# Cross samples' third and fourth key fetches a step sooner, and projection weights from the fifth pair on loaded by ScalarE's queue

## The chip, the cores and the metric

The kernel runs on one core of a Trainium2 chip. The metric is the device time of one execution in microseconds (us). A run of the kernel before takes 1438.98 us (median of three, 1438.52 to 1439.62). One execution was profiled; the views quoted below are all of that one.

The engines are named as the profile names them: PE (TensorE, matrix products), PEld (its weight loads), DVE (VectorE), ACT (ScalarE), POOL (GpSimd) and SP (SyncE). SPq and ACTq stand for the instructions with which SP and ACT issue DMA transfers. Each engine works through its own list in order and waits at the head of it: an instruction that waits holds everything behind it on its engine, DMA issues included.

## The reference

One inference step of one mixer layer, for a prompt group (1 x 1024 tokens) and a sample group (8 x 1 token) with the same weights, all in float32. Cut to what matters here:

```python
h = rmsnorm(x, norm_gain)
proj = h @ w_in                                   # 1024 x 10256, one combined input projection
q, k, v, gla_g, a_lr, u, pool_g, xq, xg, merge = split(proj)
o, S = gla_chunked(q, k, v, log_a, S0)            # branch A: gated linear attention, 4 heads
br_gla = rmsnorm(o, gla_gain) * silu(gla_g)
br_pool = multiscale_pool(u, ...) * silu(pool_g)  # branch B: trailing means of 2/4/8/16 tokens
# branch C: cross-attention, 4 heads of 256, into 256 memory tokens
s = einsum('bthd,bmhd->bhtm', xq, mk) / 16
br_x = einsum('bhtm,bmhd->bthd', softmax(s), mv) * silu(xg)
y = sum_n(sigmoid(merge_n) * (branch_n @ w_branch[n])) @ w_out
out = rmsnorm(x + y, final_gain)
```

For the prompt, `mk` and `mv` are made from `mem_prompt`. For the 8 samples the keys and values come from a cache (`cache_mem_k`, `cache_mem_v`: 8 samples x 256 tokens x 4 heads x 256), so each sample has its own keys.

## The kernel before, in words

**The projection.** `w_in` is worked through in 40 `pairs` of 2 x 128 columns. A pair is one block product by Strassen's scheme with seven products, numbered j = 0 to 6: 11, 12, s2, s1, s3, s4 and 22 are the seven left operands, made from the four quarters a11, a12, a21, a22 of the pair's weights. Every float32 operand is split in a high part `h` (made by ACT) and a low part `l` (made by DVE: the operand less its high part), and each product of two such operands takes three matmuls (L242, L243, L244). One product is 2 halves x 4 x 3 matmuls of 128 x 258; the order of the products is `seq`: (i,1) to (i,4), then (i+1,0), then (i,5), (i,6).

**The weights' path.** A pair's weights come in two DMA transfers of 512 KB into tiles called `raw` (`Pair.load`, L296): `lo`, the first half of the rows, has a11 and a21, and `hi` has a12 and a22. There are three such buffers for all pairs. `prepare` makes the left operands three products ahead of the one that PE is given, and places the loads: `hi` of the next pair when s3 = a11 - a21 is made (j = 4), which is the last use of the buffer it takes over, and `lo` of the pair after that when a22 has been split (j = 6). In `operands`, L305 is a DVE sum or difference of quarters; `ws<-raw` of s1 = a21 + a22 is the first DVE instruction of a pair that needs its `hi`.

**The side work.** Between the half products, `fill` lets a stream of side work run: cross-attention (`cross_steps`), then gated linear attention, then pooling. Each step yields a cost, and `fill` goes on until the costs so far have caught up with the place in the projection (493 units over the slots 28 to 357, of two for each product). The side work's products go to the PSUM tiles `pz` (two buffers), the projection's to `px` (six).

**The cross samples.** For each head h, `cross_sample` first makes the scores of the 8 samples on DVE (L768, `kc<-kc,qb`: the cached keys times a query that is spread over all partitions). Keys (`kc`, four buffers) and queries (`qb`, four) are fetched for two samples at a time by `cross_keys`: fetches 0 and 1 at the end of the head before, fetch 2 after sample 2's scores (b = 2), fetch 3 after b = 4. Fetch 2 is used from b = 4, fetch 3 from b = 6. The scores then go through PE (L777), a softmax whose result is `ps` (L779, L784), PE again (L795, L804 with the cached values `vc`) and so on. The same stream carries the prompt's cross-attention: query chunks `xq` (fetched by SP, split at L226 and L227), scores, `nm` (L709), `p`, and its transposes (L724).

**What sets the order.** PE's and SP's lists stand in the order in which the program is written. DVE's, ACT's and POOL's are laid by a scheduler; `tc.issue_after(x)` makes what follows stand behind x on the same engine. In the kernel before all these loads and fetches (`raw`, `xq`, `kc`, `qb`, `vc`) are in SP's one list.

Of the kernel before, what the change touches and what calls it, by code (L numbers as in the profile page):

```python
# [18 lines left out]
P = 128  # L19
# [28 lines left out]
def trunk_kernel(ctx: ExitStack, tc: tile.TileContext,  # L48
# [3 lines left out]
    nc = tc.nc  # L52
# [13 lines left out]
    def exp_ln_table():  # L66
        load = nc.scalar.add_instruction(mybir.InstLoadActFuncSet(
            act_func_set_id=EXP_LN_SET, name=nc.get_next_instruction_name(), engine=nc.scalar.engine,
            ins=[], outs=[]))
        for i in table["others"]:  # L70
            tc.add_manual_dep(load.ins, i.ins.name, nosync, reason="table set")
        table["load"], table["others"] = load, []

    def act(out, x, func, **kw):
        i = nc.scalar.activation(out, x, func, **kw)
        if func in (AF.Sigmoid, AF.Silu):
            table["others"].append(i)
            for e in table["exps"]:
                tc.add_manual_dep(i.ins, e.ins.name, nosync, reason="table set")
        else:  # L80
            tc.add_manual_dep(i.ins, table["load"].ins.name, nosync, reason="table set")
            table["new"].append(i)
        return i
# [15 lines left out]
    def PZ():  # L99
        return ps.tile([P, 512], F32, tag="pz", name="pz", bufs=2)  # L100
# [13 lines left out]
    def R(shape, dt=F32, name="r"):  # L114

        return shaped(wk.tile([P, 512], dt, tag="ring", name=name, bufs=NR), shape)
# [7 lines left out]
    def RAW(name):  # L124
        return wk.tile([P, 4, CT], F32, tag="raw", name=name, bufs=3)
# [7 lines left out]
    def tiny(w, name="t", bufs=8):  # L133
        return wk.tile([P, 16], F32, tag="t", name=name, bufs=bufs)[:, :w]
# [83 lines left out]
    last = {}  # L218
# [68 lines left out]
    class Pair:  # L287
# [3 lines left out]
            self.src, self.dst, self.s0, self.gated, self.raw = src, dst, s0, gated, [None, None]  # L291
            self.turned = turned

        def load(self, i):
            raw = RAW("raw")
            nc.sync.dma_start(out=raw, in_=self.src.rearrange("(k p) n -> p k n", p=P)[:, 4 * i:4 * i + 4])  # L296
            self.raw[i] = raw

        def operands(self):
# [26 lines left out]
    pairs = []  # L326
# [8 lines left out]
    NPAIR = len(pairs)  # L335
# [7 lines left out]
        seq += [(i, 5), (i, 6)]  # L343
    RIGHT = ("11", "21", "t2", "t1", "t3", "22", "t4")
    AHEAD = 3
    left, prep = {}, {"n": 0}

    def prepare(n):

        while prep["n"] < min(n + 1, len(seq)):  # L350
            i, j = seq[prep["n"]]
            p = pairs[i]
            if j == 0:
                p.gen = p.operands()
            left[i, j] = next(p.gen)

            if (i, j) == (0, 1):
                pairs[1].load(0)
            if j == 4 and i + 1 < NPAIR:
                pairs[i + 1].load(1)  # L360
            elif j == 6 and i + 2 < NPAIR:
                pairs[i + 2].load(0)
            prep["n"] += 1

# [303 lines left out]
    def loaded(src, shape, name, alloc=None):  # L668
        t = (alloc or R)(shape, name=name)
        nc.sync.dma_start(out=t, in_=src)  # L670
        return t

    def column0(t, d):

        return t.rearrange("p (i d j r) -> p i d j r", i=2, d=2, j=4)[:, :, d, :, 0]

    def perm8(ap):
        return ap.rearrange("p (i j) -> p i j", i=2)
# [60 lines left out]
    def cross_scaled(h):  # L739
        xs = wk.tile([P, 16], F32, tag="xsq", name="xsq", bufs=2).rearrange("p (i b) -> p i b", i=2)  # L740
        nc.vector.tensor_scalar(xs, smp_of(S_XQ + 2 * h, 2), 1.0 / 16.0, None, op0=ALU.mult)
        cross["xs", h] = xs

    def cross_rows(h):

        xs = cross["xs", h]
        t = PZ()
        for i in range(2):
            nc.tensor.transpose(t[:NS, i * P:(i + 1) * P], xs[:, i], ident)
        qn = R([DV], name="qn")  # L750
        nc.scalar.activation(qn[:NS], t[:NS, :DV], AF.Copy)
        nc.gpsimd.dma_start(out=xq_scr[h], in_=qn[:NS])

    def cross_keys(h, b2):
        kc = [loaded(ck[2 * b2 + bb, :, h, :].rearrange("(a p) d -> p a d", p=P), [2, DV], "kc", V) for bb in range(2)]
        qb = [wk.tile([P, DV], F32, tag=t, name="qb", bufs=2) for t in ("alc", "st")]
        for bb in range(2):
            nc.sync.dma_start(out=qb[bb], in_=xq_scr[h][2 * b2 + bb].partition_broadcast(P))
        cross["kc", h, b2] = kc, qb

    def cross_sample(h):

        sc = wk.tile([P, 16], F32, tag="sc", name="sc", bufs=2)
        for b in range(NS):
            kcs, qb = cross["kc", h, b // 2]
            kc = kcs[b % 2]
            for a in range(2):
                nc.vector.tensor_tensor_reduce(kc[:, a, :], kc[:, a, :], qb[b % 2],  # L768
                                               scale=1.0, scalar=0.0, op0=ALU.mult, op1=ALU.add,
                                               accum_out=sc[:, a * NS + b:a * NS + b + 1])  # L770
            if b in (2, 4):
                cross_keys(h, b // 2 + 1)
            yield 0.7
        yield 0.5
        t = PZ()
        for a in range(2):
            nc.tensor.transpose(t[:NS, a * P:(a + 1) * P], sc[:, a * NS:(a + 1) * NS], ident)  # L777
        nm = tiny(1, "nm")[:NS]
        nc.vector.tensor_reduce(nm, t[:NS, :NM], axis=AX.X, op=ALU.max, negate=True)  # L779
        p = R([NM], name="ps")[:NS]  # L780
        sm = tiny(1, "sm")[:NS]
        act(p, t[:NS, :NM], AF.Exp, bias=nm, accum_out=sm)
        nc.vector.reciprocal(sm, sm)
        nc.vector.tensor_scalar(p, p, sm, None, op0=ALU.mult)  # L784

        def own_values(i):
            return [loaded(cv[4 * i + j, :, h, :].rearrange("(a p) d -> p a d", p=P), [2, DV], "vc", V) for j in range(4)]

        vc = own_values(0)
        if h + 1 < NH:  # L790
            cross_scaled(h + 1)
        yield 1.5
        t = PZ()
        for a in range(2):
            nc.tensor.transpose(t[:, a * NS:(a + 1) * NS], p[:, a * P:(a + 1) * P], ident[:NS, :NS])  # L795
        nc.vector.tensor_copy(pm[:, :, :, 0], t[:, :2 * NS].rearrange("p (a b) -> p a b", a=2))
        yield 1.2
        yield 0.5
        cs = R([2, DV], name="cs")
        for i in range(2):  # L800
            t = PZ()
            for a in range(2):
                for j in range(4):
                    nc.tensor.matmul(t[32 * j:32 * j + 32, :DV], lhsT=pm[:, a, 4 * i + j, :], rhs=vc[j][:, a, :],  # L804
                                     start=a == 0, stop=a == 1)
            nc.scalar.activation(cs[:, i], t[:, :DV], AF.Copy)
            if i == 0:
                vc = own_values(1)
                yield 2.2
                yield 0.5  # L810
                if h + 1 < NH:
                    cross_rows(h + 1)
                yield 1.2
                yield 0.5
        if h + 1 < NH:
            cross_keys(h + 1, 0)
        yield 2.2
        if h + 1 < NH:
            cross_keys(h + 1, 1)
        yield 0.5  # L820
        t = PZ()
        for i in range(2):
            for d in range(2):
                nc.tensor.transpose(t[:, (2 * i + d) * P:(2 * i + d + 1) * P], cs[:, i, d * P:(d + 1) * P], ident)
        for d in range(2):
            nc.vector.tensor_copy(perm8(brs[2][:, 2 * h + d]), column0(t, d))
        yield 1.2
        yield 0.5

    def cross_steps():  # L830
# [10 lines left out]
        def values(n):  # L841
            cross_values(n // 4, n % 4)

        samples = chain_of(cross_sample(h) for h in range(NH))
        cross_load(0)
        cross_fetch(0, 0)
# [412 lines left out]

    def emit(n, ahead=AHEAD):  # L1260
        prepare(n + ahead)
        if seq[n] == (28, 0):
            streams[0].rest()
            other_table()
        elif seq[n] == (36, 0):
            streams[1].rest()
        for _ in run_product(n):
            fill()
# [38 lines left out]
    with tc.issue_after(last["hi"].ins), tc.issue_after(last["lo"].ins):  # L1307
        prepare(0)
# [6 lines left out]
    with tc.issue_after(last["hi"].ins), tc.issue_after(last["lo"].ins):  # L1315
        prepare(1)
        for j in (4, 6):
            r = squares(x_t[j:j + 2], 4 + j)
            scaled(x_t[j], r[:, 0:1])
            scaled(x_t[j + 1], r[:, 1:2], True)  # L1320
        prepare(3)
# [163 lines left out]
    for hf, order in enumerate(ORDERS):  # L1485
        for tb in order:
# [23 lines left out]
            n, a = hf, 0  # L1510
            for b in ends:
# [14 lines left out]
                n, a = n + 1, b  # L1526
# [46 lines left out]
```

## Time and profile before

| what | value |
|---|---|
| median of three runs | 1438.98 us |
| the profiled execution | 1438.66 us, of which 1436.6 us from the first instruction to the last |
| PE busy | 1412.3 us (98%) |
| DVE, ACT, POOL busy | 913.3 us (64%), 677.7 us (47%), 221.6 us (15%) |
| granted TensorE clock | 0.998 |
| DMA: SP's and ACT's queue rows | 183.87 MB and 0.20 MB |

The page divides the span in 40 slices; PE stands at 9 (90% or more) in all but the first and the last. The projection's pairs lie between some 25 and 1060 us, the cross-attention between some 110 and 370 us. A busy PE is modelled: each matmul is drawn longer than the distance to the next, so a short wait can be hidden by the drawn end of the matmul before it.

### The profile page before, as it was taken

The numbers are of one execution on the slowest core, as the hardware profiler recorded it, in microseconds if no ns is written. First come the engines' busy times: TensorE is split into PE (matmuls) and PEld (weight loads), VectorE is DVE, ScalarE is ACT, GpSimd is POOL, SyncE is SP. The second block draws the span as 40 slices with busy tenths as digits, with TensorE's granted clock in tenths as the row PEclk, the third lists the DMA queues.
The fourth block names the chain that finished last, engine by engine and source line by source line (L and its number), as shares of the span: only waits on it lengthen the run. The fifth ranks groups of instructions, "written<-read, shape, count | busy, mean of one in ns | idle before, by whom it ended". The sixth has DMA issues, their size and how long they took to land.

```text
span 1436.6 us, 28221 instructions
## 1 busy us (share of the span) xinstructions
PE 1412.3 (98%) x10689; PEld 1352.1 (94%) x10689; DVE 913.3 (64%) x2123; ACT 677.7 (47%) x1575; POOL 221.6 (15%) x401
## 2 busy tenths in 40 slices
PE   7999999999999999999999999999999999999998
PEld 6899988999999999999999999999999999999876
DVE  6956655767687777867766777776572534554436
ACT  6744434444565656566544445444472422333222
POOL 3212101125342121121221111110010000000000
PEclk9999999999999999999999999999999999999999
DMA  9357566656555554543654555554684777632633
GB/s 334 123 164 233 187 206 187 225 177 188 156 151 183 163 184 134 177 148 122 205 156 141 164 175 171 168 186 156 212 289 143 227 264 253 226 104 80 221 121 117
DMA packets 185812, 259.43 MB, mean 181 GB/s; under 512 B 22460, under 2 KB 136916, under 8 KB 185668
## 3 DMA queue, kind: packets, MB, share of 16 engines
q1 hardware_dynamic: 162204, 183.87, 41.3%
q0 software_dynamic: 23328, 73.56, 14.8%
q8 instruction: 84, 1.38, 0.4%
q14 instruction: 52, 0.43, 0.1%
q10 hardware_dynamic: 144, 0.20, 0.0%
HBM read 180.47 MB, written 77.56 MB: 180 GB/s over the span
## 4 chain that ended last, share of the span: by engine, by line
PE 82%; DVE 1%; ACT 0%; issue 0%; DMA 0%; DVEq 0%; ACTq 0%
PE px L242 24%; PE px L243 24%; PE px L244 24%; PE pz L242 2%; PE pz L243 2%; PE pz L244 2%; PE pz L970 1%; PE pz L951 1%; PE pz L953 1%; PE pz L914 0%; PE pz L804 0%; PE pz L724 0%; PE pz L1055 0%; PE px L1493 0%; DMA raw<-in_w_in_dram 0%
## 5 line engine op out<-in xcount | busy, mean ns | idle before, releaser
L244 PE MATMUL px<-bh,wbl 128*128 128x384 f32 (+1 forms) x576 | 184.1, 320 | 0.0
L243 PE MATMUL px<-bl,wbh 128*128 128x384 f32 (+1 forms) x576 | 184.1, 320 | 0.0
L242 PE MATMUL px<-bh,wbh 128*128 128x384 f32 (+1 forms) x576 | 183.7, 319 | 0.0
L554 ACT ACTIVATE r<-px 128x258 f32<-128x258 f32 x240 | 90.2, 377 | 45.5 <-PE px L244 44.9
L242 PEld LDWEIGHTS px<-bh,wbh 128*128 128x128 f32 x576 | 108.3, 188 | 0.0
L243 PEld LDWEIGHTS px<-bl,wbh 128*128 128x128 f32 x576 | 108.2, 188 | 0.0
L244 PEld LDWEIGHTS px<-bh,wbl 128*128 128x128 f32 x576 | 108.2, 188 | 0.0
L242 PE MATMUL px<-o,a12h 128*128 128x258 f32 x320 | 92.9, 290 | 0.8 <-DVE c L645 0.8
L242 PE MATMUL px<-ot,s3h 128*128 128x258 f32 x320 | 93.6, 292 | 0.0
L242 PE MATMUL px<-o,s4h 128*128 128x258 f32 x320 | 93.2, 291 | 0.2 <-DVE c L636 0.2
L242 PE MATMUL px<-ot,s1h 128*128 128x258 f32 x320 | 93.3, 291 | 0.0
L242 PE MATMUL px<-o,a11h 128*128 128x258 f32 x320 | 92.7, 290 | 0.0
L242 PE MATMUL px<-ot,a22h 128*128 128x258 f32 x320 | 92.4, 289 | 0.0
L242 PE MATMUL px<-ot,s2h 128*128 128x258 f32 x320 | 92.2, 288 | 0.0
L243 PE MATMUL px<-o,a11h 128*128 128x258 f32 x320 | 91.0, 284 | 0.3 <-DVE o L224 0.3
L243 PE MATMUL px<-ot,s2h 128*128 128x258 f32 x320 | 90.1, 282 | 0.5 <-DVE ot L224 0.5
L244 PE MATMUL px<-o,a11l 128*128 128x258 f32 x320 | 90.6, 283 | 0.0
L243 PE MATMUL px<-ot,a22h 128*128 128x258 f32 x320 | 90.5, 283 | 0.0
L244 PE MATMUL px<-ot,s1l 128*128 128x258 f32 x320 | 90.4, 283 | 0.0
L244 PE MATMUL px<-ot,s3l 128*128 128x258 f32 x320 | 90.4, 283 | 0.0
L244 PE MATMUL px<-o,a12l 128*128 128x258 f32 x320 | 90.4, 283 | 0.0
L243 PE MATMUL px<-o,a12h 128*128 128x258 f32 x320 | 90.4, 283 | 0.0
(471 smaller groups left out, 4622.2 us busy)
## 6 DMA issues: line engine op xcount, KB each, us to landing
raw<-in_w_in_dram SPq DMA_DIRECT2D x80, 512.0 KB, 4.0
msc<-c POOLq DMA_DIRECT2D x24, 516.0 KB, 4.7
brsc<-c POOLq DMA_DIRECT2D x24, 516.0 KB, 3.8
sig<-msc SPq DMA_DIRECT2D x24, 516.0 KB, 6.2
brr<-brsc SPq DMA_DIRECT2D x48, 256.0 KB, 5.0
wbr<-in_w_branch_dram SPq DMA_DIRECT2D x24, 512.0 KB, 5.5
acc<-sig POOLq DMA_DIRECT2D x16, 516.0 KB, 4.9
acc<-acc SPq DMA_DIRECT2D x16, 516.0 KB, 7.2
```

Of the source, the lines that this page charges most:

```text
L242: nc.tensor.matmul(out, lhsT=lh, rhs=rh, start=start, stop=False, skip_group_check=more)
L243: nc.tensor.matmul(out, lhsT=lh, rhs=rl, start=False, stop=False, skip_group_check=more)
L244: nc.tensor.matmul(out, lhsT=ll, rhs=rh, start=False, stop=stop, skip_group_check=more)
L554: nc.scalar.activation(r, acc[c][:, :QT], AF.Copy)
L951: nc.tensor.matmul(t[0:64, 0:P], lhsT=ki[:, 0:64], rhs=qi, start=True, stop=True)
L953: nc.tensor.transpose(t[:, P:2 * P], kt, ident)
L970: nc.tensor.matmul(to, lhsT=kiqi[:, 1, cs], rhs=st, start=False, stop=True)
```

## The change

Two things. First, from pair 4 on (the fifth) the loads of `raw` are issued by ACT instead of SP: `hi` behind the high part of s3, at the same step of `prepare` as before (j = 4), and `lo` behind the high part of a12 of the following pair (j = 1) instead of at the end of the pair before (j = 6), which is one step of `seq` later. That moves 72 of the 80 loads. Second, fetches 2 and 3 of a head's sample keys are placed after b = 1 and b = 3 instead of after 2 and 4, and one of the pauses of the step list moves from the end of the eight samples to between b = 3 and b = 4; with the last sample's cost raised from 0.7 to 1.2, a head's costs grow by 0.5 units, 2 units in all.

```diff
-        def load(self, i):
+        def load(self, i, queue=nc.sync):
             raw = RAW("raw")
-            nc.sync.dma_start(out=raw, in_=self.src.rearrange("(k p) n -> p k n", p=P)[:, 4 * i:4 * i + 4])
+            queue.dma_start(out=raw, in_=self.src.rearrange("(k p) n -> p k n", p=P)[:, 4 * i:4 * i + 4])
             self.raw[i] = raw
...
     AHEAD = 3
+    FIRST_ON_ACT = 4
...
             if (i, j) == (0, 1):
                 pairs[1].load(0)
-            if j == 4 and i + 1 < NPAIR:
+            if i + 1 < NPAIR and j in (1, 4) and i + 1 >= FIRST_ON_ACT:
+                with tc.issue_after(last["hi"].ins):
+                    pairs[i + 1].load(j // 4, nc.scalar)
+            elif j == 4 and i + 1 < NPAIR:
                 pairs[i + 1].load(1)
-            elif j == 6 and i + 2 < NPAIR:
+            elif j == 6 and i + 2 < FIRST_ON_ACT:
                 pairs[i + 2].load(0)
...
-            if b in (2, 4):
-                cross_keys(h, b // 2 + 1)
-            yield 0.7
-        yield 0.5
+            if b in (1, 3):
+                cross_keys(h, b // 2 + 2)
+            yield 0.7 if b < 7 else 1.2
+            if b == 3:
+                yield 0.5
```

SP's list, where the second head's sample keys are fetched (the queries of that head are `xqs_125`). Before:

```order
L670 DMA kc<-in_cache_mem_k_dram 128x2x256 x2
L758 DMA qb<-xqs_125 128x256 x2
L296 DMA raw<-in_w_in_dram 128x4x256
L670 DMA kc<-in_cache_mem_k_dram 128x2x256 x2
L758 DMA qb<-xqs_125 128x256 x2
L296 DMA raw<-in_w_in_dram 128x4x256
L670 DMA xq<-xqsc_171 128x2x256
L670 DMA kc<-in_cache_mem_k_dram 128x2x256 x2
L758 DMA qb<-xqs_125 128x256 x2
L670 DMA kc<-in_cache_mem_k_dram 128x2x256 x2
L758 DMA qb<-xqs_125 128x256 x2
```

And SP's list there now:

```order
L674 DMA kc<-in_cache_mem_k_dram 128x2x256 x2
L762 DMA qb<-xqs_125 128x256 x2
L674 DMA kc<-in_cache_mem_k_dram 128x2x256 x2
L762 DMA qb<-xqs_125 128x256 x2
L674 DMA xq<-xqsc_171 128x2x256
L674 DMA kc<-in_cache_mem_k_dram 128x2x256 x2
L762 DMA qb<-xqs_125 128x256 x2
L674 DMA kc<-in_cache_mem_k_dram 128x2x256 x2
L762 DMA qb<-xqs_125 128x256 x2
```

The two weight loads have left; the query chunk `xq` still stands ahead of fetches 2 and 3.

ACT's list a little later, where the high parts of pair 5's s3 and pair 6's a11 are made. Before:

```order
L655 ACTIVATE c_2610<-px 128x258 x2
L223 ACTIVATE s3h<-ws 128x512
L736 ACTIVATE xo<-pz 128x512
L223 ACTIVATE pTh<-pz 128x512
L223 ACTIVATE a11h<-raw 128x512
L554 ACTIVATE r_2794<-px 128x258
```

ACT's list there now:

```order
L659 ACTIVATE c_2608<-px 128x258 x2
L223 ACTIVATE s3h<-ws 128x512
L296 DMA raw<-in_w_in_dram 128x4x256
L740 ACTIVATE xo<-pz 128x512
L223 ACTIVATE pTh<-pz 128x512
L223 ACTIVATE a11h<-raw 128x512
L558 ACTIVATE r_2790<-px 128x258
```

The load of pair 6's `hi` stands behind s3h and ahead of the evacuations that follow.

DVE's list where pair 4's first sum (`ws<-raw`, which needs that pair's `hi`) stands beside the first head's sample softmax (`ps`). Before:

```order
L619 TENSOR_TENSOR c_1934<-px,r_1779 128x258
L779 TENSOR_REDUCE nm<-pz 8x1
L305 TENSOR_TENSOR ws<-raw 128x512
L783 RECIPROCAL sm<-sm 8x1
L784 TENSOR_SCALAR ps<-ps,sm 8x256
L619 TENSOR_TENSOR c_1934<-px,r_1815 128x258
L224 TENSOR_TENSOR a11l<-raw,a11h 128x512
L709 TENSOR_REDUCE nm<-pz 128x2
```

DVE's list there now:

```order
L623 TENSOR_TENSOR c_1934<-px,r_1777 128x258
L784 TENSOR_REDUCE nm<-pz 8x1
L788 RECIPROCAL sm<-sm 8x1
L789 TENSOR_SCALAR ps<-ps,sm 8x256
L623 TENSOR_TENSOR c_1934<-px,r_1813 128x258
L224 TENSOR_TENSOR a11l<-raw,a11h 128x512
L305 TENSOR_TENSOR ws<-raw 128x512
L713 TENSOR_REDUCE nm<-pz 128x2
```

The sum that needs the weights has moved behind `ps`, the second `c` and a11l; the `nm` of the prompt still stands behind it.

On PE the numbers and kinds of instructions are as before (10060 rows); the side work's matmuls stand none to two half products later.

## The prediction

> **What bounds the kernel now.** I read the busy times first.
>
> ```profile
> PE 1412.3 (98%) x10689; PEld 1352.1 (94%) x10689; DVE 913.3 (64%) x2123; ACT 677.7 (47%) x1575; POOL 221.6 (15%) x401
> ```
>
> PE is the bound, and the change leaves its instructions as they are. So all that can be won is the time in which PE stands still, 1436.6 - 1412.3 = 24.3 us, and all that can be lost is new standstill. Next I read the waits of PE, in stretches of 50 us from 100 us on (the first load that moves is issued near 135 us). Columns: waiter, releaser, us in total, times, longest. The first five rows are of 200 to 250 us, then one each of 150 to 200, 350 to 400 and 700 to 750 us.
>
> ```profile
> PE pz L724 <- ACT p L75: 1.2, 1, 1.2
> PE pz L795 <- DVE ps L784: 1.2, 1, 1.2
> PE pz L242 <- ACT p L75: 1.1, 1, 1.1
> PE px L242 <- DVE c L645: 0.8, 1, 0.8
> PE pz L777 <- ACT xo L736: 0.7, 1, 0.7
> ...
> PE pz L242 <- ACT p L75: 0.8, 1, 0.8
> ...
> PE pz L1008 <- DVE ak L224: 0.6, 1, 0.6
> ...
> PE pz L1070 <- ACT os L1064: 1.3, 1, 1.3
> ```
>
> Five of the eight lie together between 207 and 226 us: 1.2 + 1.2 + 1.1 + 0.8 + 0.7 = 5.0 us. What is lost is somewhat more than shown, as the timeline of PE at the first of them tells:
>
> ```profile
> 207.05 0.28 PE L243 MATMUL pz<-pTl,mvsh 128*128 128x256 f32 x1
> 207.17 0.28 PE L244 MATMUL pz<-pTh,mkv 128*128 128x256 f32 x1
> 208.28 0.39 PE L242 MATMUL px<-o,a12h 128*128 128x258 f32 x1 [0.83 <-DVE c L645]
> ```
>
> Matmuls follow each other after 0.12 us but are drawn 0.28 us long, so each wait hides 0.16 us under the drawn end: five of them are 5.0 + 0.8 = 5.8 us.
>
> Why are five releasers late at once? The timelines of SP and then of DVE say it.
>
> ```profile
> 185.59 1.17 SPq L758 DMA_DIRECT2D qb<-xqs  x2
> 196.69 0.38 SPq L296 DMA_DIRECT2D raw<-in_w_in_dram  x1
> 197.17 0.53 SPq L670 DMA_DIRECT2D xq<-xqsc  x1
> 197.75 1.22 SPq L670 DMA_DIRECT2D kc<-in_cache_mem_k_dram  x2
> 199.02 1.39 SPq L758 DMA_DIRECT2D qb<-xqs  x2
> ...
> 189.10 0.08 DVE L768 DVE_READ_ACCUMULATOR2_ANT sc<- 128x1 f32 x1
> 195.97 0.69 DVE L224 TENSOR_TENSOR a22l<-raw,a22h 128x512 fp32r<-128x512 f32 x1
> 206.50 0.42 DVE L768 CUSTOM_DVE_ANT_0 kc<-kc,qb 128x256 f32<-128x256 f32 x1 [7.21 <-DMA qb<-xqs]
> 213.54 0.68 DVE L305 TENSOR_TENSOR ws<-raw 128x512 f32<-128x512 f32 x1
> 219.50 0.69 DVE L305 TENSOR_TENSOR ws<-raw 128x512 f32<-128x512 f32 x1 [2.92 <-DMA raw<-in_w_in_dram]
> ```
>
> From 186.8 to 196.69 us SP stands before one weight load, whose buffer comes free only when a22l is done (195.97 + 0.69 = 196.66). Behind it stand `xq` and the second head's key fetch 2, whose buffers were free when sample 1's scores ended at 189.18. So the fetch is issued at 197.75 to 200.4, and DVE stands 7.21 us in front of sample 4. All that DVE makes after that is late (the s3 sum at 213.54, with it the next `hi`, at which DVE stands another 2.92 us), and PE meets it five times. Over the whole run, SP's and DVE's waits:
>
> ```profile
> SPq L296 <- DVE a22l L224: 162.8, 20, 12.6
> SPq L296 <- DVE ws L305: 138.7, 20, 10.7
> ...
> DVE ws L305 <- DMA raw<-in_w_in_dram: 24.7, 20, 3.0
> DVE kc L768 <- DMA qb<-xqs: 16.6, 9, 7.2
> ```
>
> SP stands some 300 us before weight loads in these two rows alone, yet little of it reaches PE: most fetches behind have time.
>
> **The change part by part.** *The sample keys' fetch at 197 us.* With the weight load gone, `xq` is next in SP's list; it needs the buffer of an earlier chunk, read last by these matmuls. The second row is the `qb` transfers' time from issue to landing.
>
> ```profile
> L244 PE MATMUL pz<-mkTh,xq x4: 279/283/283, 188.4 to 189.5; 128*128 128x256 f32 x4
> ...
> DMA to landing us min/median/max: 3.1/5.6/6.2
> ```
>
> The buffer is free at 189.5 + 0.28 = 189.8 us. Then `xq` 0.53, `kc` 1.22, `qb` 1.39 us of issue: 192.9 us, landing at 198.5. DVE came to sample 4 at 206.50 - 7.21 = 199.3. The 7.21 us wait goes, and with it the lateness of 207 to 226 us. Fetch 3, now behind b = 3, follows within 3 us, and is used two samples later. The bounds: 5.8 us if all five waits go; 2 if `xq` or a later raw stands in the way for half of the time. What is late next there is the `hi` load (below), so I take 5.0.
>
> *The `hi` loads, 36 of them, on ACT.* Here, one quiet pair in SP's, DVE's and ACT's timelines, then the times to landing of all raw loads, and ACT's only DMA issue in the run before:
>
> ```profile
> 953.19 0.38 SPq L296 DMA_DIRECT2D raw<-in_w_in_dram  x1
> 964.34 0.38 SPq L296 DMA_DIRECT2D raw<-in_w_in_dram  x1
> ...
> 963.62 0.68 DVE L305 TENSOR_TENSOR ws<-raw 128x512 f32<-128x512 f32 x1
> 969.35 0.69 DVE L305 TENSOR_TENSOR ws<-raw 128x512 f32<-128x512 f32 x1 [2.35 <-DMA raw<-in_w_in_dram]
> 969.96 0.42 DVE L619 TENSOR_TENSOR c<-px,r 128x258 f32<-128x258 f32 x1
> 970.30 0.68 DVE L224 TENSOR_TENSOR a11l<-raw,a11h 128x512 fp32r<-128x512 f32 x1
> ...
> 956.04 0.63 ACT L223 ACTIVATE a12h<-raw 128x512 fp32r<-128x512 f32 x1 [2.44 <-PE px L243]
> 965.16 0.37 ACT L75 ACTIVATE c<-px 128x258 f32<-128x258 f32 x1
> 967.55 0.63 ACT L223 ACTIVATE a11h<-raw 128x512 fp32r<-128x512 f32 x1 [2.02 <-issue]
> ...
> DMA to landing us min/median/max: 3.6/4.0/11.8
> ...
> 1432.86 0.37 ACTq L1535 DMA_DIRECT2D out_dram<-yl  x1
> ...
> 734.27 0.69 DVE L305 TENSOR_TENSOR ws<-raw 128x512 f32<-128x512 f32 x1 [1.35 <-DMA raw<-in_w_in_dram]
> ```
>
> SP issues `hi` the moment the s3 sum ends (964.34). ACT can only do so behind s3h and, in most pairs, one evacuation `c`: 965.53, which is 1.2 us later. This speaks against the change: where SP was free, the load now lands later, and DVE, which stood 2.35 us before the sum that needs it, would stand longer. But the scheduler has put a `c` and a11l, 0.42 + 0.68 = 1.1 us, ahead of that sum in many pairs. So the further wait is 0.1 us in a pair with the new order and 1.2 without; I take 0.3 as the mean, 36 x 0.3 = 11 us of DVE. How much of that reaches PE? Of the 24.7 us in the run before, I count two as felt by PE outside the cluster. One is the row at 734.27, behind which `os` came late (1.3 us). The other is the 0.8 us row at 157 us, where `ps` and `nm` stood behind such a sum in DVE's list. With the hidden 0.16 these are 1.5 + 1.0 = 2.5 us, a tenth. So +1.1 us; bounds 0 and 36 x 1.2 x 0.1 = 4.3.
>
> *The `lo` loads, 36, on ACT.* They go from 953.19 to behind a12h, some 957 us. Used by a11h at 967.55, so 957 + 4.0 leaves 6 us of cover: nothing, and nothing unless the landing exceeds 10 us. The new wait on ACT, for a22l, is past by then (SP's issue at 953.19 marks it). Queued behind it on ACT are px evacuations; if DVE lagged by over 3 us, PE would follow.
>
> *ACT's issue time.* 72 x 0.37 = 26.6 us on an engine with 1436.6 - 677.7 = 759 us idle. PE's waits on ACT above are 1.2 + 1.1 + 0.7 + 0.8 + 1.3 = 5.1 us for 677.7 busy, under 1%: +0.2 us, bounds 0 and 26.6.
>
> *The three lone waits.* Each can go or stay. At 157 us (1.0) DVE's list now has `ps` ahead of the sum that waits for `hi`, but the `nm` that p needs still stands behind: -0.5. At 740 us (1.5) the load lands later but the reader L1070 stands two half products later too: -0.5. At 389 us (0.8) the backlog is not SP's: -0.3. Bounds 0 and -3.3.
>
> *Pace.* Two more units of 493 move side work by none to two half products, with the same matmuls: nothing in itself.
>
> Sum: -5.0 + 1.1 + 0.2 - 0.5 - 0.5 - 0.3 = -5.0 us. The profiled execution took 1438.66, so 1433.7; the median of the runs is 0.3 above it: **1434.0 us**.
>
> The Trainium skill has a rule against this: by "DMA: Bandwidth & Descriptors", section "Issuing engines are not separate DMA queues", transfers started from several engines share the same DMA engines, and one saves only the issuing time, usually small. By that rule the sum would be the 72 x 0.38 us of SP, which is no bound: 1439.0. The trace bears out the small issue time, but not that it is all: SP's 9.9 us standstill before 196.69 held other transfers.
>
> **The rivals.** *No change.* A place in SP's list is all that is won, and DVE stands at the next thing instead, the later `hi`. For it: the 2.92 us wait sits right in the cluster, and 300 us of SP's waits cost PE almost nothing. Against it: sample 4's wait is 7.21 us alone, and its keys' buffers were free 8 us before. Net 0 to -2: 1438.
>
> *Slower.* The later `hi` decides. If 0.3 us of the 1.2 reached PE in each pair, 36 x 0.3 = 10.8 us, less the 6.3 won: 1443.5. It decides from 6.3 / 36 = 0.18 us a pair. For it: DVE's 2.35 us wait in a quiet pair. Against it: there PE did not notice.
>
> *More.* All eight waits go and nothing new comes: -5.8 - 3.3 = -9.1, 1429.9.
>
> **How the numbers follow.** A change of 0.2%, 2.9 us, is about what can be told from none. The forecast has 0.60 (its own range 1431.5 to 1436), no change 0.24, slower 0.11, more 0.05. Forecast and more, but for a little that falls short, are faster: 0.64; no change and that remainder: 0.26; slower: 0.10. The range from 1430.5 to 1440 leaves out most of slower and more.
>
> **What would show it.** Right: between 207 and 226 us PE has no waits; DVE's wait for `qb` falls from 16.6 us to under 6; SP issues the second head's fetch 2 near 191; raw loads on ACTq take 0.37. Wrong: PE waits for `p` or `c` behind sums that wait for raw, once per pair; DVE's wait for raw well over 35 us; ACT standing at its DMA issues; or the 7 us wait still there, behind `xq`.

## The result and the profile after

The changed kernel takes 1434.5 us (median of 13 runs, 1432.0 to 1438.1) against 1438.98 us of the kernel before (13 runs): the ratio is 0.9968, 95% interval 0.9961 to 0.9975, that is 4.6 us less. The forecast was 1434.0. The profiled execution of the changed kernel took 1435.0 us, with a span of 1433.3 (before 1436.6).

The busy times and two of the DMA queue rows of its page (packets, MB, share of 16 engines):

```profile
PE 1413.6 (99%) x10689; PEld 1354.0 (94%) x10689; DVE 916.5 (64%) x2123; ACT 679.4 (47%) x1575; POOL 220.0 (15%) x401
q1 hardware_dynamic: 124188, 146.11, 32.8%
q10 hardware_dynamic: 38160, 37.95, 9.4%
```

72 loads of 0.52 MB have gone from SP's queue to ACT's. PE's busy time is 1.3 us more, with the same instructions; that comes up again below. PE's waits from 90 to 1100 us are now:

```profile
PE pz L956 <- DVE ak L224: 2.4, 1, 2.4
PE pz L1075 <- ACT os L1069: 1.0, 1, 1.0
PE pz L244 <- DVE xq L227: 0.7, 2, 0.5
```

None of the five waits of 207 to 226 us ("the cluster" from here on) is left, nor the one at 157 us. The first row is new; it stands at 537 us. SP's timeline where the second head's key fetch 2 is issued:

```profile
188.92 0.53 SPq L674 DMA_DIRECT2D xq<-xqsc  x1
189.54 1.06 SPq L674 DMA_DIRECT2D kc<-in_cache_mem_k_dram  x2
190.66 0.93 SPq L762 DMA_DIRECT2D qb<-xqs  x2
```

Fetch 2 starts at 189.54 instead of 197.75, 8.2 us sooner. Of DVE's waits, the two that the prediction showed, and the `raw` loads that ACT issues (duration least, median, most; first and last start):

```profile
DVE ws L305 <- DMA raw<-in_w_in_dram: 21.0, 14, 4.9
DVE kc L772 <- DMA qb<-xqs: 10.7, 10, 2.6
...
L296 ACTq DMA_DIRECT2D raw<-in_w_in_dram x72: 374/374/463, 137.7 to 1023.3; - x72
```

DVE's longest wait for `qb` is 2.6 us (7.2 before). Its waits for `raw` have become fewer (14 for 20), but one is 4.9 us long. The chain of waits at the new standstill of PE, start and length of each piece, and the row of that window (PE, PEld, DVE, ACT, POOL busy; granted clock; DMA share; GB/s):

```profile
522.81 0.63 ACT s3h L223
523.44 0.12 ACT c L659
523.56 9.38 DMA raw<-in_w_in_dram
...
533.03 0.06 DVE ws L305
...
539.68 0.35 DVE ak L224
...
540.16 0.29 PE pz L956
...
541.01 0.22 PE px L242
...
543.80 0.21 PE px L243
544.02 0.12 PE px L244
```

```profile
536.00:546.00 10.00, 7.54 (x49) 7.16 (x50) 7.08 (x22) 6.55 (x19) 0.71 (x1) 0.83 0.44 137
```

A `hi` load that ACT issues behind s3h and one `c` takes 9.38 us to land; DVE's sum waits for it, and behind the sum stands DVE's chain to `ak`, for which PE waits. Then, from 541.0 to 543.8 us, the matmuls follow each other in 0.21 us instead of 0.12: the granted clock in that window is 0.83.

The balance of the two profiled executions, each standstill as the distance from one matmul to the next less the usual 0.12 us: the cluster 5.9 us less (0.99 + 1.38 + 0.84 + 1.38 + 1.28), 157 us 0.9 less, 388 us 0.4 less, 738 us 0.3 less; new are 2.6 us at 537, 1.5 us lost in the slow matmuls behind it (against the same matmuls in another execution of this kernel, where none of them is slow), and a smaller one of 0.25 us before it. Together -3.2; the spans differ by 3.3.

### The profile page after: what moved, and what is told of

The parts are those of the page before. It is cut to its first block, busy times and chain, and to the rows that moved or that the text cites. A ratio compares the mean times of both kernels' runs of the same rounds, so it can differ in the third digit from the quotient of the medians.

```text
span 1433.3 us, 28230 instructions
## 1 busy us (share of the span) xinstructions
PE 1413.6 (99%) x10689; PEld 1354.0 (94%) x10689; DVE 916.5 (64%) x2123; ACT 679.4 (47%) x1575; POOL 220.0 (15%) x401
## 3 DMA queue, kind: packets, MB, share of 16 engines
q8 instruction: 84, 1.38, 0.4%
## 4 chain that ended last, share of the span: by engine, by line
PE 93%; DVE 3%; DMA 2%; ACT 1%; issue 1%; DVEq 0%; SPq 0%; ACTq 0%
PE px L242 27%; PE px L243 26%; PE px L244 26%; PE pz L244 3%; PE pz L242 3%; PE pz L243 3%; DMA raw<-in_w_in_dram 2%; PE pz L975 1%; PE pz L408 1%; PE pz L956 1%; PE pz L809 1%; PE pz L958 1%; PE pz L728 0%; PE pz L919 0%; DVE ot L224 0%
## 5 line engine op out<-in xcount | busy, mean ns | idle before, releaser
L242 PE MATMUL px<-ot,s1h 128*128 128x258 f32 x320 | 93.1, 291 | 0.0
L243 PE MATMUL px<-ot,s1h 128*128 128x258 f32 x320 | 90.3, 282 | 0.0
```

The costliest lines, as they stand in the source:

```text
L242: nc.tensor.matmul(out, lhsT=lh, rhs=rh, start=start, stop=False, skip_group_check=more)
L243: nc.tensor.matmul(out, lhsT=lh, rhs=rl, start=False, stop=False, skip_group_check=more)
```

## The experiments

Theory A, from the prediction: SP stood before one load (pair 6's `lo`) with the second head's keys behind it; take that load out of SP's list, and the cluster goes. Rival B: it is the sooner fetches. Rival C: DVE stands at the next thing instead. Each kernel was timed against the kernel before on the same chip:

| kernel | median, us | ratio to before (95%) | in us |
|---|---|---|---|
| the change | 1434.5 | 0.9968 (0.9961 to 0.9975) | -4.6 |
| one load moved | 1433.2 | 0.9959 (0.9946 to 0.9972) | -5.9 |
| loads on ACT alone | 1435.9 | 0.9972 (0.9961 to 0.9982) | -4.0 |
| fetches and pauses alone | 1442.6 | 1.0022 (1.0013 to 1.0030) | +3.2 |
| change, only `hi` on ACT | 1446.9 | 1.0053 (1.0039 to 1.0066) | +7.6 |
| pauses alone | 1446.5 | 1.0046 (1.0033 to 1.0059) | +6.6 |
| change without the pauses | 1436.3 | 0.9969 (0.9957 to 0.9981) | -4.5 |
| only `hi` loads on ACT | 1440.3 | 0.9997 (0.9989 to 1.0005) | -0.4 |
| only `lo` loads on ACT | 1435.1 | 0.9968 (0.9956 to 0.9980) | -4.6 |
| pauses alone, one load moved | 1439.0 | 0.9993 (0.9983 to 1.0003) | -1.0 |
| change, only `lo` on ACT | 1431.8 | 0.9947 (0.9935 to 0.9960) | -7.6 |
| two loads moved | 1435.1 | 0.9967 (0.9954 to 0.9979) | -4.7 |
| the change again | 1432.3 | 0.9953 (0.9940 to 0.9967) | -6.8 |

The last column is the ratio times the median before of that batch (1438.98, 1439.39, 1440.5 and 1439.29 us). Its intervals are about 2 us to either side; smaller differences between two kernels decide nothing. The first row is a batch of its own; the next four, the four after those and the last four are one batch each. The same kernel, the change, came out at -4.6 in the first batch and at -6.8 in the last, so a difference of 2 to 3 us between rows of different batches decides nothing either.

### One load moved

```diff
-            elif j == 6 and i + 2 < NPAIR:
+            elif j == 6 and i + 2 < NPAIR and i + 2 != 6:
                 pairs[i + 2].load(0)
+            elif (i, j) == (5, 1):
+                with tc.issue_after(last["hi"].ins):
+                    pairs[6].load(0, nc.scalar)
```

> The kernel before with one single load moved: pair 6's lo is issued by ACT behind the high part of a12 of pair 5, all other loads, the key fetches and the pace as before. Theory A (SP stood before this one load, with the second head's keys behind it): the five waits of PE between 207 and 226 us go, 5.8 us, so 1438.9 falls to 1433 to 1434.5; SP issues the query chunk near 190 and fetch 2 by 193; DVE's longest wait for qb falls from 7.2 to under 3 us. Rival B (the sooner fetches are what wins): no change, 1438 to 1439.5, DVE's wait stays above 5 us. Rival C (DVE stands at the next thing instead, the hi load of the 2.92 us row): 1437 to 1438.5.

SP's timeline and DVE's wait for `qb` over the run:

```profile
190.33 0.53 SPq L673 DMA_DIRECT2D xq<-xqsc  x1
190.96 1.06 SPq L673 DMA_DIRECT2D kc<-in_cache_mem_k_dram  x2
192.07 0.93 SPq L761 DMA_DIRECT2D qb<-xqs  x2
...
DVE kc L771 <- DMA qb<-xqs: 10.4, 9, 2.1
```

PE has no wait between 200 and 250 us. One of 80 loads, moved to another list, wins 5.9 us (4.0 to 7.8), which is no less than the whole change. Theory A holds at this place; B and C do not explain it.

### Loads alone, fetches and pauses alone, only `hi`

Loads on ACT, with the fetches and pauses of before:

```diff
-            if b in (1, 3):
-                cross_keys(h, b // 2 + 2)
-            yield 0.7 if b < 7 else 1.2
-            if b == 3:
-                yield 0.5
+            if b in (2, 4):
+                cross_keys(h, b // 2 + 1)
+            yield 0.7
+        yield 0.5
```

> The loads on ACT as in the change, the key fetches after b = 2 and 4 and the pace as before. SP's list at the second head's keys is the same as in the changed kernel. Theory A: the cluster goes here too, 1433.5 to 1435.5, and the difference to the changed kernel is under 1.5 us. Rival B (sooner fetches): 1438 to 1440, with the cluster still there. If the ACT loads cost what was taken for them (1.3 us), it comes out above the kernel with one load moved.

Fetches and pauses of the change, all loads on SP:

```diff
-    FIRST_ON_ACT = 4
+    FIRST_ON_ACT = NPAIR
```

> The sooner key fetches and the pace as in the change, all loads on SP as before. In SP's list the load of pair 6's lo still stands ahead of the query chunk and fetch 2 of the second head. Theory A: SP still stands until a22l, the cluster stays, 1437.5 to 1439.5. Rival B: fetches a sample sooner are worth the gain alone, 1433.5 to 1435.

The change with the `lo` loads back on SP:

```diff
-            if i + 1 < NPAIR and j in (1, 4) and i + 1 >= FIRST_ON_ACT:
+            if j == 4 and i + 1 < NPAIR and i + 1 >= FIRST_ON_ACT:
                 with tc.issue_after(last["hi"].ins):
-                    pairs[i + 1].load(j // 4, nc.scalar)
+                    pairs[i + 1].load(1, nc.scalar)
...
-            elif j == 6 and i + 2 < FIRST_ON_ACT:
+            elif j == 6 and i + 2 < NPAIR:
```

> The changed kernel with only the hi loads on ACT; the lo loads stay on SP where they were, so pair 6's lo again stands ahead of the query chunk and fetch 2. Theory A: the cluster stays and the hi loads cost their 1.1 us: 1438 to 1441. Rival (any load that leaves SP helps, half of the gain each): 1436 to 1437. The price of hi on ACT is read against the kernel with the sooner fetches alone.

The first came out as theory A has it: no wait between 200 and 250 us, -4.0 us, and 0.6 us from the change; its median of 1435.9 is 0.4 above the range. The other two missed on the slow side, and for another reason than either theory. In the second, SP stands before the load as foreseen, and DVE still waits 4.5 us in front of sample 4:

```profile
195.28 0.38 SPq L296 DMA_DIRECT2D raw<-in_w_in_dram  x1
195.76 0.61 SPq L674 DMA_DIRECT2D xq<-xqsc  x1
...
203.79 0.43 DVE L772 CUSTOM_DVE_ANT_0 kc<-kc,qb 128x256 f32<-128x256 f32 x1 [4.51 <-DMA qb<-xqs]
```

But of the cluster only one wait of 0.8 us is left, so the claim that it stays was wrong. The shifted side work and the sooner fetches together leave little of that delay; with the pauses alone (below) one standstill of 1.9 us is left there. The loss is elsewhere, in waits of PE that no prediction had, here of the second kernel and the third:

```profile
PE pz L1139 <- DMA hist<-in_state_pool_dram: 4.9, 1, 4.9
PE pz L956 <- DVE ak L224: 2.1, 2, 1.3
```

```profile
PE pz L1139 <- DMA hist<-in_state_pool_dram: 4.7, 1, 4.7
PE pz L956 <- DVE ak L224: 2.7, 2, 2.5
```

The state `hist` of the pooling, fetched by SP near 742 us, is late. So a new question: is that the pauses' doing, and is it the same mechanism?

### Pauses alone

```diff
-            yield 0.7
-        yield 0.5
+            yield 0.7 if b < 7 else 1.2
+            if b == 3:
+                yield 0.5
```

> The kernel before with only the pauses of the change (2 units more over four heads); loads and key fetches as before. Theory A2 (from the kernel with the sooner fetches alone, where the cluster went too, but hist came 5 us late at 742 us and new waits stood at 540 and 633): the shifted side work makes those late waits, so they show here: a wait near 540 us of 1.4 us or more, the hist wait of some 5 us near 742; with the cluster still partly there, 1440 to 1444. Rival (the sooner fetches make them): the waits of before at their places, none near 540, 1438 to 1440.

It is the slowest but one, +6.6 us, and 2.5 us above the top of the range. SP's and PE's timelines:

```profile
717.25 26.49 SPq L296 DMA_DIRECT2D raw<-in_w_in_dram  x3
743.85 0.45 SPq L674 DMA_DIRECT2D pwr<-in_pool_w_dram  x1
744.39 0.43 SPq L1128 DMA_DIRECT2D hist<-in_state_pool_dram  x1
...
748.72 0.99 PE L1139 MATMUL pz<-sel,hist 120*128 120x8 f32 x4 [4.92 <-DMA hist<-in_state_pool_dram]
...
750.16 0.42 PE L243 MATMUL px<-ot,s3h 128*128 128x258 f32 x1
```

Three loads stand in a row in SP's list, and to issue them takes 26.5 us: SP stands 11.6 and 13.6 us before two of them, until the DVE instructions that free their buffers are done. In the kernel before there are two at this place: the pauses move the side work (and with it `hist`) behind one more load, pair 27's `lo`. The wait near 540 us that was expected did not come here; that part of the theory was wrong. The last row is drawn 0.42 us long instead of 0.28, since a slow stretch follows here too. The two windows, with the same columns as above (granted clock 0.88 and 0.78):

```profile
740.00:750.00 10.00, 4.23 (x29) 3.56 (x28) 2.97 (x10) 2.44 (x5) 1.57 (x5) 0.88 0.73 200
750.00:760.00 10.00, 10.00 (x69) 10.00 (x69) 5.57 (x19) 3.09 (x7) 1.28 (x2) 0.78 0.25 80
```

### Pauses alone, with one load moved

```diff
+            elif (i, j) == (26, 1):
+                with tc.issue_after(last["hi"].ins):
+                    pairs[27].load(0, nc.scalar)
-            elif j == 6 and i + 2 < FIRST_ON_ACT:
+            elif j == 6 and i + 2 < FIRST_ON_ACT and i + 2 != 27:
```

> The kernel with only the pauses of the change, and one load of it moved: pair 27's lo, the third load in the row before which SP stood from 717 to 744 us with hist behind it, is issued by ACT. Theory A2 (SP's one list: a load that waits for its buffer holds what stands behind): hist is issued some 11 us sooner, near 732, the 5.0 us wait at 743 us goes and with it the stretch of slow matmuls behind it (2.0 us), so 5 to 8 us below the kernel with the pauses alone: 1438.5 to 1441.5. Rival (hist is late by the shifted side work itself): the wait stays over 3 us, less than 2 us won.

```profile
719.19 12.29 SPq L296 DMA_DIRECT2D raw<-in_w_in_dram  x2
731.58 0.47 SPq L677 DMA_DIRECT2D pwr<-in_pool_w_dram  x1
732.13 0.44 SPq L1131 DMA_DIRECT2D hist<-in_state_pool_dram  x1
```

`hist` leaves 12.3 us sooner, the wait is gone, and the kernel falls from +6.6 to -1.0 us: 7.6 us for one load, as far as two batches can be compared. It is theory A at a second place, and it says what the two parts of the change have to do with each other: the pauses alone cost 6.6 us as long as the loads are in SP's list, and nothing that can be measured without them, which the next kernel shows.

### The change without the pauses

The loads on ACT and the sooner fetches, with the pauses of before (the diff of "pauses alone", backwards).

> The changed kernel with the pauses of before: all loads on ACT and the sooner fetches stay. Theory A2: the 2.6 us wait near 537 us goes, the cluster stays away, so it stands within 1 us of the kernel with only the loads on ACT, 1433.5 to 1436. Rival (the wait near 537 is the late hi load's, 9.4 us on its way): the wait stays, at 1.5 us or more.

-4.5 us (the median is 0.3 us above the range), as the change itself (-4.6) and as the loads alone (-4.0): with all these loads gone from SP, neither pauses nor fetches make a difference that can be measured. The 2.6 us wait near 537 us is gone, so it needs the pauses, and the rival falls. Instead PE stands 2.7 us at 733 us, as in the kernel with the loads alone, which reads there:

```profile
PE pz L1074 <- ACT os L1068: 2.6, 1, 2.6
```

### Only `hi`, only `lo`, with fetches and pauses of before

Both have the same diff as "only `hi`" above or its counterpart (`j == 1`, `load(0, nc.scalar)`, and `hi` on SP at j = 4), on the kernel before.

> The kernel before with only the hi loads of pairs 4 to 39 on ACT; lo loads, key fetches and pauses as before. Pair 6's lo still stands ahead of the second head's fetch 2, so theory A keeps the cluster, or most of it: 1437 to 1440.5, of which 0 to 4.3 us is the price of the later hi (1.1 taken). Against theory A: below 1435.5.

> The kernel before with only the lo loads of pairs 4 to 39 on ACT; hi loads, key fetches and pauses as before. Theory A: the cluster goes, as with the one load alone, and the other 35 lo loads cost nothing: 1432.5 to 1435, within 1 us of the kernel with one load moved. If the spread of the runs comes from ACT's hi loads, its runs lie as close together as those of that kernel (3 us).

With only `hi` on ACT the cluster stays, in PE's and DVE's waits of that stretch:

```profile
PE pz L728 <- ACT p L75: 1.2, 1, 1.2
PE pz L799 <- DVE ps L788: 1.2, 1, 1.2
PE pz L242 <- ACT p L75: 1.1, 1, 1.1
PE pz L781 <- ACT xo L740: 0.7, 1, 0.7
...
DVE kc L772 <- DMA qb<-xqs: 7.7, 2, 6.8
```

The `hi` loads do two things that cancel: the wait at 157 us (0.9) and one of the cluster's go, and the wait for `os` at 737 us grows from 1.5 to 2.7 us. With only `lo` on ACT there is no wait between 200 and 250 us, and 4.6 us are won, 1.3 less than with the one load, which is within the intervals: the other 35 cost nothing that can be measured. Its five runs lie within 2.8 us, as expected, and the twelve with only `hi` within 5.6. But the change without the pauses, with `hi` on ACT, has 2.7, and the kernel with the pauses and one load moved, without it, 6.3: that the `hi` loads make the spread is not shown.

### The change with only `lo` on ACT, and the change again

```diff
-            if i + 1 < NPAIR and j in (1, 4) and i + 1 >= FIRST_ON_ACT:
+            if j == 1 and i + 1 < NPAIR and i + 1 >= FIRST_ON_ACT:
                 with tc.issue_after(last["hi"].ins):
-                    pairs[i + 1].load(j // 4, nc.scalar)
+                    pairs[i + 1].load(0, nc.scalar)
```

> The changed kernel with the hi loads back on SP: only the lo loads are on ACT; sooner fetches and pauses stay. Theory A2: no load that waits for a22l stands in SP's list, so neither the cluster nor the hist wait comes, 1432.5 to 1436; the wait near 537 us shrinks or goes if it is the hi load behind s3h on ACT (then 2 to 3 us below the changed kernel), and stays at 1.5 us or more if it is the pauses' doing.

> The changed kernel once more, unaltered, beside the other three on the same chip, for the wait near 537 us. If the transfer of 9.4 us ahead of it was a chance of that one execution, the wait differs by over 1 us; if it belongs to the kernel's order, it stands again at 2 to 3 us. Time 4 to 5 us below the kernel before, and over the kernels that move one or two loads by 0.5 to 2 us.

In the change run again the wait near 537 us is there once more, and a `hi` load is again long on its way ahead of it (7.84 us, in the chain of waits):

```profile
PE pz L956 <- DVE ak L224: 1.3, 1, 1.3
...
523.79 7.84 DMA raw<-in_w_in_dram
```

This time PE stands 1.4 us, no slow stretch follows, and the execution is 2.8 us shorter (1432.2 after 1435.0). The place belongs to the kernel's order; the size differs by 1.2 us, which by the expectation's own mark is the chance of one execution. The time missed too: 6.8 us below the kernel before, not 4 to 5, and below the kernel with two loads moved, not over it.

With `hi` back on SP there is no wait of PE from 500 to 550 us, so in the change it takes both, the pauses and `hi` behind s3h on ACT. A late `hi` is not the only way to it: the kernel with fetches and pauses alone, with every load on SP, stood 1.4 us at the same instructions at 540 us (the first of its two waits for `ak` above), behind another transfer that took long:

```profile
526.54 7.47 DMA vb<-vs
```

The kernel with only `lo` on ACT was the fastest of all, 7.6 us below the kernel before, and 0.7 us below its range. That it beats the change again (6.8 us below, in the same batch) lies within the intervals. It is also 3.0 us below "only `lo`" with the fetches and pauses of before, but those are two batches, so it stays open whether fetches and pauses win something there.

### Two loads moved

One load moved, and pair 4's `hi` on ACT as well:

```diff
+            if (i, j) == (3, 4):
+                with tc.issue_after(last["hi"].ins):
+                    pairs[4].load(1, nc.scalar)
-            if j == 4 and i + 1 < NPAIR:
+            elif j == 4 and i + 1 < NPAIR:
```

> The kernel with one load moved, and one more: pair 4's hi is issued by ACT too, behind the high part of s3. With it the sum that needs this load stands behind the sample softmax (ps) in DVE's list, as in the changed kernel. Expected: the 1.4 us wait of PE at 157 us shrinks to 0.4 or less, the rest as with one load, so about 1 us below that kernel, 5.5 to 7 us below the kernel before. Rival (the wait at 157 is not this sum's): no difference to the kernel with one load.

The wait at 157 us went, as expected, since DVE's order there is now that of the change; but a wait of 1.3 us came at 219 us, and the time is 4.7 us below before and not lower than with one load. A miss in the sum: a wait won was given back 60 us later.

## Why the prediction was right

**The cluster, -5.0.** Measured -5.9 (the bound if all five go was 5.8). Cause and place hold: one load at the head of SP's list (one load moved: the five waits go and the time falls by 5.9; only `hi` moved: four of the five stay). It was said that SP would issue fetch 2 near 191: 189.5. It was also said that DVE's wait for `qb` would fall to under 6 us in all: it is 10.7, in ten pieces, of which the longest is 2.6. That mark was set wrong: with these ten pieces there, PE has no wait from 200 to 250 us.

**The `hi` loads, +1.1, bounds 0 and 4.3.** The mechanism, 0.3 us more of DVE's standing in each of 36 pairs, did not show: DVE's wait for `raw` fell from 24.7 to 21.0 us. The cost comes in one place, 2.6 + 1.5 = 4.1 us at 537 us in the one execution and 1.4 in the other. Kernels that differ only by `hi` on ACT are 0.9 us apart (the change again against the change with only `lo`, within the intervals), 0.6 us (the loads alone against only `lo`, within them), 4.4 us (only `hi` in the change against fetches and pauses alone, outside them), and 0.4 us in favour of `hi` (only `hi` on the kernel before, within them). So a price per pair was the wrong form: where a late transfer meets a chain that PE waits for decides, and the order of the side work sets that.

**ACT's issue time, +0.2, and the `lo` loads, 0.** 72 x 0.374 = 26.9 us of issue, and none of the waits of PE shown above is put down to them; the 36 `lo` loads on ACT leave the time where one of them puts it.

**The lone waits, -1.3.** Measured -0.9 at 157 us, -0.3 at 738 and -0.4 at 388: -1.6.

**Pace, 0.** The size was right by luck, and the reason wrong. The two units are worth +6.6 us with the loads on SP. They cost nothing here only because the other half of the change takes those loads away, and because, in the profiled executions, the wait that they bring at 537 us stands in place of one of 2.7 us at 733 us. The prediction looked for what the pauses change on PE, where the matmuls stay the same, and not for what they move past in SP's list.

**The sum, -5.0.** In the profiled execution the cluster (-5.9) and the lone waits (-1.6) won 1.2 us more than forecast, and the `hi` loads with the pauses (+4.1) cost 3 us more. In the change run again the wait at 537 us cost 1.4 us, not 4.1. So the median is 0.5 us from the forecast for the cluster's sake, which was understood, and because errors of opposite sign cancel, which is luck.

**The rule of the Trainium skill,** that only the issuing time is saved ("DMA: Bandwidth & Descriptors", "Issuing engines are not separate DMA queues"), gives 1439.0 here; the runs disagree with it as a sum for this kernel. Moving one load, 0.38 us of issue, was worth 5.9 us, and another one 7.6, since a list that waits for a buffer holds the transfers behind it.

**The rivals.** "No change", with DVE standing at the next thing, falls by the kernel with one load moved. "Slower", by the later `hi`, is real in size only where `hi` meets the shifted side work. "More" asked for -9.1; the change run again, -6.8 us, lies between it and the forecast.

**What stays open.** The runs of the change spread over 6 us in the first batch and 3.5 in the last; that the wait near 537 us and its slow stretch vary fits, but two profiled executions do not settle it. Why the sooner fetches win 3.4 us when the pauses and SP loads are there (+3.2 against +6.6) is only half told by the one standstill of 1.9 us at 212 us and its slow stretch of 1.5, which they take away, since three others of 0.8 to 1.4 us (159, 220 and 540 us) come with them. Every kernel that moves the one load puts it behind the fetches and into another engine's list at once; whether a place behind the fetches in SP's own list would win the same wasn't tried, nor was a fourth buffer for `raw`, which could take away the waits themselves.

## What to carry to other kernels

Look in each DMA-issuing list for the instruction that waits longest, and at what stands behind it: a transfer whose buffer was long free and whose reader is on the way to the bound engine was worth far more here (5.9 us) than the issue time (0.38 us), and moving the one waiting load can win as much as moving all of them. A shift of work by a step is not free because its engine does the same instructions: see in every in-order list what it is moved past. And price a late transfer by the place where the bound engine meets it, not by an average per iteration.

## What the runs showed of the hardware

A standstill of PE can cost more than itself. In the fourteen traces, from 90 to 1340 us, nine of the eleven standstills of 1.9 to 5.1 us were followed by a slow stretch in which the matmuls came at 0.21 us instead of 0.12. The granted clock there is 0.50 (0.83 and 0.78 in the windows shown above, which are longer than the stretch). It lasts 3.41 us, and twice that behind the three standstills of 4.8 us and more. Against the same matmuls in a kernel without it, a stretch of 3.41 us cost 1.5 us (four pairs, 1.47 to 1.54).

Behind the standstills of 1.7 us and less there was none. Two of the three standstills of 2.7 us had none either, so length alone does not decide. Here are windows of 3.41 us with the columns of above: first three of the change at 537 us, then one of the change without the pauses, then two of the loads alone.

```profile
537.06:540.47 3.41, 0.98 (x10) 0.68 (x8) 3.34 (x10) 1.49 (x5) 0.00 (x0) 1.00 0.46 169
540.47:543.88 3.41, 3.41 (x19) 3.35 (x17) 2.10 (x9) 3.28 (x12) 0.00 (x0) 0.50 0.03 5
543.88:547.30 3.42, 3.42 (x29) 3.37 (x29) 1.49 (x4) 1.63 (x6) 0.71 (x1) 1.00 0.90 302
...
733.62:737.03 3.41, 0.83 (x6) 0.63 (x7) 2.48 (x8) 2.10 (x6) 2.52 (x6) 1.00 0.61 143
...
730.90:734.31 3.41, 1.98 (x17) 1.77 (x15) 2.36 (x9) 2.67 (x8) 0.97 (x2) 1.00 0.70 201
734.31:737.73 3.42, 2.27 (x18) 2.08 (x19) 1.57 (x5) 0.91 (x2) 1.54 (x5) 1.00 0.45 79
```

Within a trace the clock changes only at whole multiples of 3.41 us from its first rise near 10 us (in "pauses alone" two stretches begin at 215.19 and 747.67 us, which is 156 times 3.413 apart). The windows above are cut on these multiples. The last two kernels stood 2.7 us at the same instructions: in the first of them the standstill lies almost whole in one window (PE is busy 0.83 us of it) and a slow stretch follows; in the second it is split over two (1.98 and 2.27 us busy) and none follows. So where the standstill falls counts. A sharp bound does not come out: the busiest window with a slow stretch behind it has 1.69 us of PE drawn as busy ("pauses alone", from 211.78 us), and one without has 1.57 ("only `hi` loads on ACT", from 735.50 us).

The Trainium skill describes such a gate ("TensorE: Matmul & The Clock Gate", "Part 1: The HAM clock gate"): half rate after an idle window of about 3.4 us, in windows that run freely. The traces agree with the half rate, with the length and with the free running, but not with the bound: here a standstill of 1.9 us was enough.
